# One hybrid decoder layer: the decay and rate low-rank products as 64-row pairs, begun later

## The chip, the cores and the metric

The kernel runs on one core of a Trainium2 chip, in one launch. The metric is the device time of that launch in microseconds (us), the median of several runs. Every engine of the core has its own queue of instructions: TensorE (PE, matrix products; PEld are its weight loads), VectorE (DVE), ScalarE (ACT), GpSimd (POOL) and SyncE (SP), which here mostly issues transfers (DMA). Engines wait for one another by semaphores, and each engine works its queue in order.

## The reference

One layer on 1024 tokens of 1024 channels, all in float32. Its first half mixes tokens in two branches that share one input projection:

```python
h = rms_norm(x, norm_mix_pre)
proj = h @ w_in            # r, k, v | decay down (64), rate down (64), gate down (128) | S5 input | two gates
p = token_shift(p, mu)     # p + (previous token - p) * mu
r, k, v, wd, ad, gd = split(p)
w = -softplus(-(w0 + tanh(wd) @ w2)) - 0.5
decay = exp(-exp(w))
a = sigmoid(a0 + ad @ a2)
g = sigmoid(gd) @ g2
```

`w2` and `a2` are 64 x 512, `g2` is 128 x 512: these are the three low-rank products. Decay, rate `a`, `k` and `v` drive a recurrence over tokens with a 64 x 64 state in each of 8 heads (RWKV-7); its output is normalised, gets a bonus term and is multiplied by `g`. The other branch is a diagonal complex state-space model (S5) with a gated output. Both branches are projected, merged with the two gates and projected once more; then follow a norm and the residual. The second half is a gated MLP with a causal convolution of width 3 and norms around it.

## The kernel before

The kernel holds activations with channels on the 128 partitions and tokens along the free dimension, in two halves of 512 tokens (`th` 0 and 1). A float32 product is made of three products in a reduced format: an operand is split into a high part (a cast on ScalarE) and a low part (a subtraction on VectorE), and high x high, high x low and low x high are summed in one PSUM bank (`mm3_steps`, L162). One such *step* has three products of 128 x 128 by 128 x 512. A projection tile (`inproj`, L943) is eight steps into one bank for each half of the tokens; `load_w` (L142) fetches its weights and splits them, into four buffers each for the high (`wh`) and the low part (`wl`).

Banks of the front half come from `gmp` (L95), four of them under the name `gm`. An evicted tile lies in one of four buffers `ev` (NEVA) until its store to device memory has landed.

The order of TensorE's instructions is that in which the program emits them; for the other engines and the transfers a scheduler orders instructions by priority and by when it expects them to be ready. `drive` (L185) emits that order: *lanes* (the S5 work first, the recurrence afterwards) run when a planned clock `now` has reached their due time, and in between `background` (L209) takes steps from a list of fill work. Each `yield` of a fill generator is the planned time that it adds to `now`: 0.68 for a step.

The first fill work is `mix_in` (L1122). It runs projection tile 12, which holds the decay and rate down-projections in its upper and lower 64 rows; `shifted_into` (L1080) applies the token shift, the tanh on the 64 decay rows, and splits the result into two `lx` buffers for each half. Then `rkv(0)` (L1113), three projection tiles of 16 steps each, is mixed with `lowrank` (L1095): after each third projection step one low-rank step. The decay weights are padded with 64 rows of zeros below and the rate weights with 64 rows of zeros above (L1962 to 1963), so each is a full 128-row product with the same `lx` operand: for each, four output tiles for two halves of the tokens, 16 steps in all. A decay tile is evicted by two ScalarE instructions (L1108, L1110), a rate tile by one (L1108), and stored to `TZ` or `TA`. The first low-rank step stands behind three projection steps. After it, tile 13 (the gate down-projection) and `rkv(1)`, mixed with the eight steps of the gate weights after each fourth projection step (`TG`). The rest of the fill work are `rkv(2)`, `rkv(3)`, sixteen gate tiles (`gate_tiles`, evicted at L1147), and later the merge of the branches and the output projection. The recurrence reads `TZ` and `TA` in `rwkv_front` (L641), and `TG` in `rwkv_out` (L900). Its products are 64-row ones, addressed by `HALF`, the upper and lower 64 partitions (L716, L850 and others). The output of its first 512 tokens goes through `YR` to the merge (L1196).

Of the kernel before, what the change touches and what calls it, by code (L numbers as in the profile page):

```python
# [12 lines left out]
AF = mybir.ActivationFunctionType  # L13
# [12 lines left out]
HALF = (slice(0, 64), slice(64, 128))  # L26
# [24 lines left out]
def _constants():  # L51
    c = np.zeros((128, NCST), np.float32)

    def put(name, a):
        o, n = CST[name]
        c[:, o:o + n] = a
    p = np.arange(128)
    put("ident", np.eye(128))
    s, t = (p % 64)[:, None], (p % 64)[None, :]
    put("gmask", np.where(p[None, :] < 64, s < t, s <= t))  # L60
    put("ones_bd", (p[:, None] // 64) == (p[None, :] // 64))
    put("nrow", np.broadcast_to(p[None, :], (128, 128)))
    put("smask", np.broadcast_to((np.arange(512) % 64 != 0)[None, :], (128, 512)))
    return c


class Kern:
# [1024 lines left out]
            self.split(*xs[-1], y)  # L1092
        return use

    def lowrank(self, xs, js):  # L1095

        nc = self.nc
        for j, hb, dst in js:
            w = self.load_w(self.a["w_lr"][j])
            for th in range(2):  # L1100
                for p in range(4):
                    ps = self.gmp()
                    yield from self.mm3_steps(ps, w, p, [xs[th][0]], [xs[th][1]])
                    t = self.ev()
                    if hb is None:
                        nc.scalar.copy(t, ps)
                    else:
                        nc.scalar.activation(t, ps, AF.Tanh, bias=self.hb[hb][:, p:p + 1], scale=0.5)  # L1108
                    if dst is self.TZ:
                        nc.scalar.activation(t, t, AF.Identity, bias=self.ones1, scale=1.0)  # L1110
                    nc.sync.dma_start(dst[p][:, th * 512:th * 512 + 512], t)

    def rkv(self, p):  # L1113

# [6 lines left out]

    def mix_in(self):  # L1122

        def mixed(a, b, n):

            for i, c in enumerate(a):
                yield c
                if i % n == n - 1:
                    c = next(b, None)
                    if c is not None:  # L1130
                        yield c
            yield from b
        self.load_u8(self.stored)
        xs = [[], []]
        yield from self.inproj((12, self.shifted_into(xs[0], 12)))
        yield from mixed(self.rkv(0), self.lowrank(xs[0], ((0, "w0", self.TZ), (1, "a0", self.TA))), 3)
        yield from self.inproj((13, self.shifted_into(xs[1], 13)))
        yield from mixed(self.rkv(1), self.lowrank(xs[1], ((2, None, self.TG),)), 4)
        self.mixed_in = True
        for p in (2, 3):  # L1140
            yield from self.rkv(p)
# [799 lines left out]
def _layout(i):  # L1941

    i = {k: np.asarray(v) for k, v in i.items()}
    f = {k: v[0] for k, v in i.items()}

    p = np.arange(512).reshape(4, 8, 16).transpose(0, 2, 1).reshape(-1)
    q = np.arange(f["w_in"].shape[1])
    q[14 * 128:18 * 128] = 14 * 128 + p
    f["w_in"] = f["w_in"][:, q]
    f["s5_w_glu"], f["s5_b_glu"] = f["s5_w_glu"][p][:, p], f["s5_b_glu"][p]  # L1950
    f["w_branch_s5"] = f["w_branch_s5"][p]

    def tiles(w):
        k, m = w.shape
        return np.ascontiguousarray(w.reshape(k // 128, 128, m // 128, 128).transpose(2, 1, 0, 3)).reshape(m // 128, 128, k)
    vec = {"g_mix_pre": f["norm_mix_pre"], "g_mix_post": f["norm_mix_post"], "g_ffn_pre": f["norm_ffn_pre"],
           "g_ffn_post": f["norm_ffn_post"], "b_gate": f["b_gate"], "mu": f["rwkv_shift_mu"], "w0": f["rwkv_w0"],
           "a0": f["rwkv_a0"], "k_k": f["rwkv_k_k"], "k_a": f["rwkv_k_a"], "r_k": f["rwkv_r_k"].reshape(-1),
           "lnx_w": f["rwkv_lnx_w"], "lnx_b": f["rwkv_lnx_b"], "b_glu": f["s5_b_glu"],
           "cw0": f["ffn_conv_w"][0], "cw1": f["ffn_conv_w"][1], "cw2": f["ffn_conv_w"][2], "cb": f["ffn_conv_b"]}  # L1960
    vec = np.concatenate([vec[n].reshape(-1, 128).T for n in VEC], axis=1)
    z = np.zeros((64, 512), np.float32)  # L1962
    lr = np.stack([np.concatenate([f["rwkv_w2"], z]), np.concatenate([z, f["rwkv_a2"]]), f["rwkv_g2"]])

    def dup(*xs):
        return np.stack([np.concatenate([x, x]) for x in xs])
    return {
        "x": np.ascontiguousarray(f["x"].T), "w_in": tiles(f["w_in"]), "vec": np.ascontiguousarray(vec),
        "cst": _constants(), "w_lr": lr, "w_glu": tiles(f["s5_w_glu"]),
        "w_br": np.stack([tiles(f["w_branch_rwkv"]), tiles(f["w_branch_s5"])]), "w_out": tiles(f["w_out"]),  # L1970
        "w_up": tiles(f["ffn_w_up"]), "w_down": np.ascontiguousarray(f["ffn_w_down"].reshape(FT, 128, D)),
        "s5_a": dup(f["s5_a_re"].T, f["s5_a_im"].T),
        "s5_ls": np.ascontiguousarray(np.broadcast_to(f["s5_log_step"][None], (128, 32))),
        "s5_b": dup(f["s5_b_re"].transpose(1, 0, 2), f["s5_b_im"].transpose(1, 0, 2)),
        "s5_c": dup(f["s5_c_re"].transpose(2, 0, 1), f["s5_c_im"].transpose(2, 0, 1)),
        "s5_d": np.ascontiguousarray(f["s5_d"].reshape(32, 16).T),
    }
# [19 lines left out]
```

## Time and profile before

| | |
|---|---|
| median of 3 runs | 1490.86 us (1490.47 to 1492.2) |
| span of the profiled execution, first to last instruction | 1491.1 us |
| TensorE busy | 1435.8 us (96%), 9284 products |
| VectorE busy | 1071.2 us (72%) |
| ScalarE busy | 729.8 us (49%) |
| mean granted clock of TensorE | 0.984 |
| transfers | 206.26 MB, mean 138 GB/s |

The profile gives the span of its one execution; beside it no separate time is recorded, and the runs lie within 1.1 us of it. In the profile's rows a group or instruction is named by engine, line of the program, operation and tiles (output <- inputs, with buffer numbers left out). "128*128 128x512" is a product of a 128 x 128 weight with 512 columns, "64*64" one in a quarter of the array. In a timeline a row has its start, its length (for several in a row, from the first start to the last end) and in brackets the idle time ahead of it and what ended it. Products overlap in the pipeline: the distance of two starts is what a product costs, and not its length. PEclk is the clock granted to TensorE, as a share of the full one.

### The profile page before, as it was taken

How to read it: one execution, taken by the hardware profiler on the slowest of the kernel's cores; microseconds unless marked ns; L12 is line 12 of the kernel's file. 1: busy time of each engine (PE TensorE's matmuls, PEld its weight loads, DVE VectorE, ACT ScalarE, POOL GpSimd, SP SyncE). 2: the span in 40 equal slices, each digit the busy share in tenths (PEclk: the TensorE clock that was granted, in tenths of full speed). 3: DMA queues.
4: the chain of work that ended last, by engine and by line, in shares of the span. 5: the costliest groups of instructions: out<-in, count | busy, mean ns of one | idle time of the engine just before them, and what ended most of it. 6: DMA issues, size and time to landing. Idle time of an engine off the chain costs nothing. (4 is left out here: it accounts for less than half of the span.)

```text
span 1491.1 us, 24155 instructions
## 1 busy us (share of the span) xinstructions
PE 1435.8 (96%) x9284; PEld 1176.3 (79%) x9284; DVE 1071.2 (72%) x1761; ACT 729.8 (49%) x1167; POOL 58.9 (4%) x116
## 2 busy tenths in 40 slices
PE   7999999999999989899999999999999999999996
PEld 5778888778878778677878877888888887888785
DVE  8977765665325859646597798777777777697677
ACT  7677653443324553633554455444444444443351
POOL 0000000010100110100000000000000000000001
PEclk9999999999999999899999999999999999999998
DMA  6453433633511575733374643222222227934723
GB/s 217 121 194 116 129 94 91 212 113 122 164 59 58 171 226 163 189 109 108 121 222 150 205 127 121 85 85 85 85 85 81 76 70 260 328 125 133 236 83 113
DMA packets 121284, 206.26 MB, mean 138 GB/s; under 512 B 29248, under 2 KB 35520, under 8 KB 121168
## 3 DMA queue, kind: packets, MB, share of 16 engines
q1 hardware_dynamic: 113296, 182.43, 39.2%
q0 software_dynamic: 6144, 19.99, 4.0%
q10 hardware_dynamic: 1728, 2.29, 0.4%
q8 instruction: 73, 1.20, 0.4%
q14 instruction: 43, 0.35, 0.1%
HBM read 150.14 MB, written 52.43 MB: 136 GB/s over the span
## 5 line engine op out<-in xcount | busy, mean ns | idle before, releaser
L172 PE MATMUL gm<-hh,wh 128*128 128x512 f32 x672 | 277.0, 412 | 10.5 <-DVE ev L1192 4.3
L173 PE MATMUL gm<-hl,wh 128*128 128x512 f32 x672 | 265.4, 395 | 0.0
L174 PE MATMUL gm<-hh,wl 128*128 128x512 f32 x672 | 265.2, 395 | 0.0
L156 ACT CAST wh<-wf 128x512 fp32r<-128x512 f32 x171 | 105.6, 619 | 168.3 <-PE gm L173 103.8
L157 DVE TENSOR_TENSOR wl<-wf,wh 128x512 fp32r<-128x512 f32 x171 | 116.9, 686 | 77.6 <-ACT wh L156 77.3
L172 PEld LDWEIGHTS gm<-hh,wh 128*128 128x128 f32 x672 | 127.6, 190 | 42.8 <-issue 5.9
L174 PEld LDWEIGHTS gm<-hh,wl 128*128 128x128 f32 x672 | 128.0, 190 | 28.1
L173 PEld LDWEIGHTS gm<-hl,wh 128*128 128x128 f32 x672 | 128.2, 191 | 24.7 <-issue 1.0
L1615 PE MATMUL d<-xl,wh 128*128 128x512 f32 x308 | 121.4, 394 | 3.5 <-DVE xl L227 3.5
L1614 PE MATMUL d<-xh,wh 128*128 128x512 f32 x308 | 121.4, 394 | 2.1 <-ACT xh L226 2.1
L1616 PE MATMUL d<-xh,wl 128*128 128x512 f32 x308 | 121.2, 393 | 0.0
L1440 PE MATMUL rp<-t,h 128*128 128x512 f32 x216 | 84.4, 391 | 1.6 <-ACT p L1454 1.6
L1442 PE MATMUL rp<-t,l 128*128 128x512 f32 x216 | 84.2, 390 | 0.5 <-DVE l L227 0.5
L1441 PE MATMUL rp<-t,h 128*128 128x512 f32 x216 | 84.1, 389 | 0.0
L1615 PEld LDWEIGHTS d<-xl,wh 128*128 128x128 f32 x308 | 58.6, 190 | 16.5 <-DVE xl L227 4.3
L1614 PEld LDWEIGHTS d<-xh,wh 128*128 128x128 f32 x308 | 58.5, 190 | 14.8 <-ACT xh L226 2.5
L1616 PEld LDWEIGHTS d<-xh,wl 128*128 128x128 f32 x308 | 58.6, 190 | 12.2
L226 ACT CAST h<-r 128x1024 fp32r<-128x1024 f32 x34 | 35.8, 1054 | 61.1 <-PE rp L1441 29.6
L227 DVE TENSOR_TENSOR l<-r,h 128x1024 fp32r<-128x1024 f32 x34 | 41.6, 1224 | 29.2 <-ACT h L226 27.7
L1461 DVE SCALAR_TENSOR_TENSOR y<-zv,vecs,y 128x1023 f32<-128x1023 f32 (+1 forms) x36 | 46.1, 1280 | 8.5 <-ACT y L1459 8.5
L1440 PEld LDWEIGHTS rp<-t,h 128*128 128x128 f32 x216 | 40.5, 188 | 11.2 <-ACT p L1454 2.5
L1454 ACT COPY p<-rp 128x512 f32<-128x512 f32 x54 | 31.0, 574 | 36.5 <-PE rp L1442 36.5
(459 smaller groups left out, 3199.4 us busy)
## 6 DMA issues: line engine op xcount, KB each, us to landing
r<-in_w_up_dram SPq DMA_DIRECT2D x36, 512.0 KB, 3.7
wf<-in_w_in_dram SPq DMA_DIRECT2D x62, 256.0 KB, 3.1
st<-in_w_down_dram SPq DMA_DIRECT2D x55, 256.0 KB, 4.1
st<-ACT SPq DMA_DIRECT2D x44, 256.0 KB, 4.5
wf<-in_w_up_dram SPq DMA_DIRECT2D x36, 256.0 KB, 2.9
ACT<-y POOLq DMA_DIRECT2D x18, 512.0 KB, 2.9
GT<-ev SPq DMA_DIRECT2D x32, 256.0 KB, 2.6
wf<-in_w_br_dram SPq DMA_DIRECT2D x32, 256.0 KB, 2.9
```

Of the source, the lines that this page charges most:

```text
L156: nc.scalar.copy(h[:, :n], f[:, :n])
L157: nc.vector.tensor_tensor(l[:, :n], f[:, :n], h[:, :n].bitcast(F32), ALU.subtract)
L172: mm(ps, a, xh[k], start=k == 0, stop=False)
L173: mm(ps, a, xl[k], start=False, stop=False)
L174: mm(ps, b, xh[k], start=False, stop=k == n - 1)
L1440: mm(ps, wh[:, c], xh, start=first and k == 0, stop=False, skip_group_check=True)
L1441: mm(ps, wh[:, c], xl, start=False, stop=False, skip_group_check=True)
L1442: mm(ps, wl[:, c], xh, start=False, stop=k == 3, skip_group_check=True)
L1461: V.scalar_tensor_tensor(y[:, lag:], z[:, 0:1024 - lag], self.vec(nme, i), y[:, lag:], ALU.mult, ALU.add)
L1614: mm(ps, wh[:, c], xh[:, x], start=start, stop=False, skip_group_check=True)
L1615: mm(ps, wh[:, c], xl[:, x], start=False, stop=False, skip_group_check=True)
L1616: mm(ps, wl[:, c], xh[:, x], start=False, stop=stop, skip_group_check=True)
```

## The change

The decay and rate weights stand in one 128 x 512 tile, decay in the upper 64 rows and rate in the lower ones, with no zeros. For each of the eight output tiles two banks are taken, and six products of 64 rows go out in turn to the upper and the lower half of the array: high x high for decay, high x high for rate, then the two other kinds. Both results are then evicted as before, by the function `lowrank_out`. A pair is planned at 0.9 us instead of two steps of 0.68. One weight tile less is loaded. In `mixed`, the low-rank generator is first taken at step 8 of the projections, where it loads its weights and gives no product; its products come after every third projection step from step 16 on, so the first one stands behind 19 projection steps (before: 3). The gate-rank products follow the same pattern (before: every fourth step from the start).

```diff
-    def lowrank(self, xs, js):
+    def lowrank_out(self, ps, hb, dst, p, th):
 
         nc = self.nc
...
+        t = self.ev()
+        if hb is None:
+            nc.scalar.copy(t, ps)
+        else:
+            nc.scalar.activation(t, ps, AF.Tanh, bias=self.hb[hb][:, p:p + 1], scale=0.5)
+        if dst is self.TZ:
+            nc.scalar.activation(t, t, AF.Identity, bias=self.ones1, scale=1.0)
+        nc.sync.dma_start(dst[p][:, th * 512:th * 512 + 512], t)
+
+    def lowrank_pair(self, xs):
+
+        mm = self.nc.tensor.matmul
+        (wh,), (wl,) = self.load_w(self.a["w_lr"][0])
+        yield 0
+        for th in range(2):
+            xh, xl = xs[th]
+            for p in range(4):
+                ps = self.gmp(), self.gmp()
+                o = slice(p * 128, p * 128 + 128)
+                for n, (a, b) in enumerate(((wh, xh), (wh, xl), (wl, xh))):
+                    for k, sl in enumerate(HALF):
+                        mm(ps[k], a[sl, o], b[sl], start=n == 0, stop=n == 2)
+                yield 0.9
+                self.lowrank_out(ps[0], "w0", self.TZ, p, th)
+                self.lowrank_out(ps[1], "a0", self.TA, p, th)
+
+    def lowrank(self, xs):
+
+        w = self.load_w(self.a["w_lr"][1])
+        yield 0
+        for th in range(2):
+            for p in range(4):
+                ps = self.gmp()
+                yield from self.mm3_steps(ps, w, p, [xs[th][0]], [xs[th][1]])
+                self.lowrank_out(ps, None, self.TG, p, th)
...
-        def mixed(a, b, n):
+        def mixed(a, b, lead, n):
 
             for i, c in enumerate(a):
                 yield c
-                if i % n == n - 1:
+                if i == lead // 2 or i >= lead and (i - lead) % n == n - 1:
...
-        yield from mixed(self.rkv(0), self.lowrank(xs[0], ((0, "w0", self.TZ), (1, "a0", self.TA))), 3)
+        yield from mixed(self.rkv(0), self.lowrank_pair(xs[0]), 16, 3)
...
-        yield from mixed(self.rkv(1), self.lowrank(xs[1], ((2, None, self.TG),)), 4)
+        yield from mixed(self.rkv(1), self.lowrank(xs[1]), 16, 3)
...
-    z = np.zeros((64, 512), np.float32)
-    lr = np.stack([np.concatenate([f["rwkv_w2"], z]), np.concatenate([z, f["rwkv_a2"]]), f["rwkv_g2"]])
+    lr = np.stack([np.concatenate([f["rwkv_w2"], f["rwkv_a2"]]), f["rwkv_g2"]])
```

More of the change, by code (lines that the diff above doesn't have):

```diff
@@ L1093, in shifted_into @@
         return use
-    def lowrank(self, xs, js):
+    def lowrank_out(self, ps, hb, dst, p, th):
         nc = self.nc
[L1098 to L1111, printed above, removed]
+        t = self.ev()
[29 more added lines that the diff above has]
+                self.lowrank_out(ps, None, self.TG, p, th)
     def rkv(self, p):
```

## Prediction

> **What bounds the kernel now.** I read the page first, then the busy time in stretches of 20 us, then the timeline of TensorE around the low-rank products. TensorE is the bound: it is busy in nearly every slice, also where the changed stage lies (slices 3 and 4 of 40, 37 us each).
>
> ```profile
> span 1491.1 us, 24155 instructions
> ...
> PE   7999999999999989899999999999999999999996
> ...
> PEclk9999999999999999899999999999999999999998
> ```
>
> Over the first 760 us it is busy for 727; the stretch from 60 to 80 us is one of the few with a hole.
>
> ```profile
> 60.00:80.00 20.00, 17.45 (x71) 13.33 (x70) 18.81 (x53) 15.77 (x22) 0.00 (x0) 0.97 0.77 211
> ...
> sum 760.00, PE 727.12 PEld 592.33 DVE 497.85 ACT 387.22 POOL 40.42; mean PE 19.13 PEld 15.59 DVE 13.10 ACT 10.19 POOL 1.06
> ```
>
> So time taken out of TensorE's own stream in the front half shifts everything behind it, as long as later work isn't waiting for something else. (The chain that ended last is followed back only through the last products of the kernel, and says nothing of this stage.) The timeline shows the hole:
>
> ```profile
> 74.20 0.39 PE L174 MATMUL gm<-hh,wl 128*128 128x512 f32 x1
> 76.50 0.51 PE L172 MATMUL gm<-lx,wh 128*128 128x512 f32 x1 [1.92 <-ACT lx L226]
> 77.52 0.50 PE L173 MATMUL gm<-lx,wh 128*128 128x512 f32 x1 [0.52 <-DVE lx L227]
> ...
> 78.80 0.63 PE L172 MATMUL gm<-hh,wh 128*128 128x512 f32 x1
> 79.22 0.63 PE L173 MATMUL gm<-hl,wh 128*128 128x512 f32 x1
> ...
> 82.20 0.40 PE L174 MATMUL gm<-lx,wl 128*128 128x512 f32 x1
> ...
> 87.24 0.39 PE L172 MATMUL gm<-lx,wh 128*128 128x512 f32 x1
> ...
> 89.96 0.39 PE L172 MATMUL gm<-lx,wh 128*128 128x512 f32 x1
> ```
>
> The rows that read `lx` are the low-rank products. From 87.24 to 89.96 lie 12 products of 512 columns: 2.72 us, so **0.227 us each and 0.68 us a step of three**. The first low-rank step stands after three projection steps of the next tile and waits for its split input. Then, from 78.80 on, products start 0.425 us apart; the granted clock says why:
>
> ```profile
> 74.60:76.50 1.90, 0.00 (x0) 0.00 (x1) 1.19 (x3) 1.85 (x4) 0.00 (x0) 1.00 0.63 254
> ...
> 78.80:82.20 3.40, 3.40 (x10) 2.63 (x8) 3.32 (x17) 0.90 (x2) 0.97 (x2) 0.50 0.42 166
> ```
>
> (columns: length, busy PE, PEld, DVE, ACT, POOL, clock, DMA share, GB/s). For 3.4 us after the wait the clock is 0.50.
>
> **The late start.** The product after 74.20 would have begun at 74.43. From there to 82.20 is 7.77 us for 14 products, which at 0.227 take 3.17: **4.6 us lost**, 3.0 to the waits and 1.6 to the clock. In the changed kernel the first low-rank product comes after 19 projection steps of the tile instead of 3, 10.9 us later, at about 72.2 + 12.9 = 85.1. Its inputs are ready by 79:
>
> ```profile
> 78.29 0.68 DVE L227 TENSOR_TENSOR lx<-ev,lx 128x512 fp32r<-128x512 f32 x1
> ```
>
> The projection steps that move ahead need their weights: those of the next tile were cast long before 72, as this row on ScalarE shows (two casts, the last two before 62).
>
> ```profile
> 59.83 1.14 ACT L156 CAST wh<-wf 128x512 fp32r<-128x512 f32 x2
> ```
>
> So I take the 4.6 us as gone. One low-rank weight load with its cast and its subtraction is gone too:
>
> ```profile
> L156 ACT CAST wh<-wf 128x512 fp32r<-128x512 f32 x171 | 105.6, 619 | 168.3 <-PE gm L173 103.8
> L157 DVE TENSOR_TENSOR wl<-wf,wh 128x512 fp32r<-128x512 f32 x171 | 116.9, 686 | 77.6 <-ACT wh L156 77.3
> ```
>
> That is 0.62 and 0.69 us on engines that were waiting for TensorE or for each other at such places, hidden by the products; uncovered it would be 1.3 us. I count nothing. The gate-rank steps (`TG`) move the same way, from every fourth step to every third behind a lead of 16; TensorE waits for `lx` nowhere but in the two rows above, and their eight stores, 5 us later in the SP queue, are read only at the output of the recurrence: nothing either way. The `TZ` and `TA` stores stay 16 and finish earlier.
>
> **The products.** Before: 16 steps of 0.68 = 10.9 us. After: 8 pairs of six 64-row products. Whether the two halves run at once, the trace shows only for narrower tiles:
>
> ```profile
> 397.17 0.27 PE L850 MATMUL cz<-V,gr 64*64 64x64 f32 x1
> 397.17 0.27 PE L851 MATMUL cz<-V,gr 64*64 64x64 f32 x1
> 397.18 0.27 PE L850 MATMUL cz<-V,gr 64*64 64x64 f32 x1
> 397.19 0.27 PE L851 MATMUL cz<-V,gr 64*64 64x64 f32 x1
> 397.27 0.22 PE L850 MATMUL cz<-V,gr 64*64 64x64 f32 x1
> ...
> 485.04 0.39 PE L174 MATMUL gm<-hh,wl 128*128 128x512 f32 x1
> 485.36 1.98 PE L716 MATMUL cz<-ar,bk 64*64 64x128 f32 x64
> 487.27 0.51 PE L172 MATMUL gm<-hh,wh 128*128 128x512 f32 x1
> 487.61 0.40 PE L173 MATMUL gm<-hl,wh 128*128 128x512 f32 x1
> ```
>
> Four products, one in each quarter of the array, start within 0.02 us, and in these lines of the code the upper and lower row halves do write the same columns, in two banks, as the new pair does. The 64 products of L716 have 128 columns each; by 0.227 us for 512 that is 0.057 us each, 3.63 us one after another, and the whole block takes 1.9. So the row halves do run at once, and the six products should take the time of three, 0.68 us. The same rows price the change between full and half rows: from 485.04 to 487.61 is 2.57 us, less two ordinary pitches 2.12, less the block at two at a time (1.81) leaves 0.3 us. A weight load of 128 columns instead of 64 is exposed with it, so I take 0.35 per pair, as eight separate blocks lie between projection steps. A pair is then 1.03 us, eight are 8.2, and the products **save 2.6 us**. Bounds: both halves at once and no price for changing, 8 x 0.68 = 5.4 us saved; one after another, 8 x (1.36 + 0.35) = 13.7 us, 2.8 lost. I stay near the first by the rows above.
>
> The Trainium skill (TensorE: Matmul & The Clock Gate, Measured speedup vs the span model) speaks for less: four row tiles of 512 columns gave 3.07 times, not four. At that share two halves give 1.54 times, an estimate of 0.88 us for the six products and 1.6 us less saved, 1486.8 in the end; L716 shows nothing of such a loss. The same page (HAM oscillation — how this bites in real kernels) lets the clock fall only after some 3.4 us of idle time; here waits of 1.92 and 0.52 us were followed by 0.50. If the rule held strictly, the 1.6 us of slow clock would have another cause and could stay, 1486.8 again; no run here shows another cause.
>
> **Evictions.** What was one eviction for each four steps is now two, issued together three steps later.
>
> ```profile
> L1072 ACT ACTIVATE ev<-gm,mu 128x512 f32<-128x512 f32 x9 | 6.2, 685 | 8.7 <-PE gm L174 4.3 <-issue 3.8 <-ACT t L569 0.5
> ...
> L1110 ACT ACTIVATE ev<-ev,ones 128x512 f32<-128x512 f32 x8 | 5.8, 724 | 0.2
> ...
> L1108 ACT ACTIVATE ev<-gm,hb_w 128x512 f32<-128x512 f32 x8 | 5.5, 682 | 1.2 <-PE gm L174 1.1
> ...
> L1108 ACT ACTIVATE ev<-gm,hb_a 128x512 f32<-128x512 f32 x8 | 5.3, 679 | 1.9 <-issue 1.9
> ```
>
> A pair costs ScalarE 0.68 + 0.72 + 0.68 = 2.08 us, in a period of three steps and a pair, 2.04 + 1.03 = 3.07. Over the eight pairs (24.6 us) ScalarE has 16.7 us of these, 3 x 0.69 for projection tiles and some 3 x 0.62 for weight casts: 20.6 of 24.6. It holds, with little to spare. A pair takes two of the four `gm` banks while a projection tile holds a third. The second bank of a pair comes free about 0.2 + 2.08 us after its last product, and the next pair wants it at 2.04; at the two pairs right behind a tile's end the old tile's bank isn't free either, and 0.69 us of its eviction may come between. That is 0 to 1.8 us; I take **0.5 us lost**, nearer the row of one eviction, where TensorE didn't wait at all. Behind it only the later projection steps would queue.
>
> **Sum up to the end of the front half:** -4.6 - 2.6 + 0.5 = -6.7 us.
>
> **Downstream.** The list of background steps is shorter by 16 x 0.68 - 8 x 0.9 = 3.7 planned us, so at each later fixed step of the recurrence about five more projection steps are already done. Where TensorE is full this changes nothing; but after the first half's output there is a place where it isn't:
>
> ```profile
> 525.76 0.60 PE L924 MATMUL rp<-csts,mt 128*128 128x128 f32 x4
> ...
> 543.95 0.50 PE L172 MATMUL gm<-hh,wh 128*128 128x512 f32 x1 [1.48 <-ACT ev L1147]
> ...
> 557.34 0.79 PE L172 MATMUL gm<-hh,wh 128*128 128x512 f32 x1 [2.70 <-ACT ev L1147]
> ```
>
> ```profile
> 533.30 0.62 ACT L226 CAST hh<-ld 128x512 fp32r<-128x512 f32 x1 [4.83 <-DMA ld<-YR]
> ...
> 539.26 1.33 ACT L226 CAST hh<-ld 128x512 fp32r<-128x512 f32 x2 [3.42 <-DMA ld<-YR]
> ...
> 543.25 0.64 ACT L1147 ACTIVATE ev<-gm,hb_b_gate 128x512 f32<-128x512 f32 x1
> ```
>
> ScalarE waits in order for the `YR` loads, which hang on the outputs of L924; the gate tile's eviction L1147 stands behind them, and TensorE waits for its bank. With 3.7 us of gate tiles already done, TensorE comes to that bank up to 3.7 us sooner against the same load. If the order on ScalarE stays, up to 3.7 us are given back; if the tile's eviction, ready sooner, goes ahead of the first wait of 4.83 us, nothing is, or the old 1.48 goes too. I take 1.0 lost (from -2 to 3.7). **Total -5.7 us**: 1491.1 - 5.7 = 1485.4 for the profiled execution, whose span is 0.2 above the median of the runs, so **1485.2** against 1490.86.
>
> **Rivals.** (1) *Given back at the output of the first half*: the full 3.7 us and one more stretch of half clock (1.6) instead of 1.0: -6.7 + 5.3, 1489.5. For it: the waits above; against it: the order on ScalarE is planned anew. (2) *The halves don't run at once*: the products lose 2.8 instead of saving 2.6, -4.6 + 2.8 + 0.5 + 1.0 = -0.3, 1490.6. Against it, the four starts within 0.02 us. (3) *Slower: the stores pace the pairs.* The four `ev` buffers are held until a store lands:
>
> ```profile
> DMA to landing us min/median/max: 2.0/3.5/5.9
> ```
>
> With landing time l a pair holds them for 2.08 + 2l, eight pairs and three projection tiles (twice 0.69 on two engines, + l each) for 21 + 19l, over four buffers 5.2 + 4.75l. At 3.5 that is 21.9 us, less than the 24.6 of the stretch. Above 4.1 every 0.1 costs 0.48 us, and the waits bring the half clock back (say twice, 3.2 us). With 7.2 won and 1.0 lost downstream the gain is used up at about 4.8, and the kernel is over 0.2% slower from 5.4 on; at the longest landing, 5.9, it is 33.2 - 24.6 + 3.2 + 1.0 = 12.8 lost against 7.2 won, 1496.5. Two stores every 3.07 us instead of one in 2.72 speak for it, a median of 3.5 against.
>
> **How the numbers follow.** Forecast (1482 to 1488) 0.58, and 0.05 for more than that (nearly free changing of modes, a lucky order downstream); rival 1 0.18; rival 2 0.07; rival 3 0.12. About 0.2%, 3 us, is what a measurement of this kernel can tell from no change. Faster is the forecast and the better tail, 0.63; within 0.2% rivals 1 and 2, 0.25; slower rival 3, 0.12. The range from 1480 to 1492.5 takes in the best products (-5.4) and rivals 1 and 2 and leaves out rival 3 and little else; the forecast's own is 1482 to 1488.
>
> **What would show it.** The low-rank pairs' rows should come in bunches with two starts together and the pair's six products within about 1.0 us; 1.7 or more is rival 2. No row on `lx` should wait for ScalarE near 75 us, and the clock from 74 to 85 should be 1.00; a wait there makes the 4.6 wrong. Waits of TensorE on `gm` for L1108 or L1110 with idle ScalarE before them are rival 3. The end of the first projection tiles should lie 6 to 7 us earlier; if it does and the kernel's end doesn't, look at the waits for L1147 between 520 and 560. A kernel within 3 us of before, or slower, makes the forecast wrong.

## The result, and the profile after

The changed kernel took 1501.83 us (median of 4 runs, 1497.72 to 1504.43) against 1491.13 of the kernel before: a ratio of **1.0071** (95% interval 1.0048 to 1.0094). It is slower by 10.7 us; 1485.2 was predicted, and 1501.83 lies above the range. The profiled execution took 1501.26 us, and its span is 1499.5 us.

The span is 8.4 us longer than the 1491.1 of before, with the same 9284 products. Where they are held up is seen in stretches of the timeline (columns: stretch, length, busy time of TensorE, its weight loads, VectorE, ScalarE and GpSimd, then TensorE's clock, DMA share, GB/s). Before:

```profile
72.00:85.00 13.00, 10.57 (x39) 7.95 (x38) 11.48 (x48) 7.15 (x11) 0.97 (x2) 0.87 0.59 176
85.00:110.00 25.00, 25.00 (x112) 20.71 (x111) 19.45 (x31) 20.71 (x34) 0.00 (x0) 1.00 0.59 197
...
540.00:590.00 50.00, 45.82 (x198) 37.11 (x198) 37.26 (x82) 29.25 (x53) 2.34 (x4) 0.93 0.61 177
...
740.00:790.00 50.00, 48.65 (x225) 40.29 (x224) 44.30 (x80) 24.75 (x43) 2.15 (x4) 1.00 0.68 211
```

The same stretches of the changed kernel:

```profile
72.00:85.00 13.00, 13.00 (x59) 10.77 (x59) 12.11 (x50) 6.57 (x12) 0.98 (x2) 1.00 0.59 183
85.00:110.00 25.00, 21.75 (x93) 14.35 (x92) 18.65 (x29) 19.15 (x30) 0.00 (x0) 0.93 0.53 181
...
540.00:590.00 50.00, 42.72 (x185) 34.65 (x184) 36.15 (x78) 28.44 (x52) 4.31 (x7) 0.93 0.60 179
...
740.00:790.00 50.00, 44.19 (x193) 36.31 (x194) 42.17 (x76) 23.68 (x42) 2.15 (x4) 0.97 0.59 189
```

The hole at the first low-rank step is closed (2.4 us more of busy time, and the full clock). Three others open: 3.3 us where the pairs now are, 3.1 us at the output of the first half of the tokens, 4.5 us at the merge. The list of TensorE's waits has a new or a grown row for each (columns: product and line, what it waited for, us in total, times, the longest):

```profile
PE gm L172 <- ACT ev L1168: 6.5, 2, 5.1
PE mm L172 <- ACT wh L156: 5.4, 1, 5.4
PE gm L1119 <- ACT ev L1102: 3.3, 3, 1.9
```

L1168 is the gate tile's eviction (L1147 before), L1119 a product of a pair, L1102 the eviction of a low-rank tile.

Three events divide the layer's first half: the first of the recurrence's 64-row products (L716), the last product of its output (L924), and the last store of the first half's normed result for the first 512 tokens (`H`), which is taken here as its end. The views of these lines give the first and the last start behind the durations. Before:

```profile
L716 PE MATMUL cz<-ar,bk x512: 268/269/321, 292.2 to 530.7; 64*64 64x128 f32 x171
...
L924 PE MATMUL rp<-csts,mt x32: 270/272/273, 511.4 to 721.6; 128*128 128x128 f32 x32
...
L1350 SPq DMA_DIRECT2D H<-tm x8: 319/323/327, 797.4 to 808.7; - x8
```

After:

```profile
L716 PE MATMUL cz<-ar,bk x512: 268/269/322, 297.1 to 533.8; 64*64 64x128 f32 x171
...
L924 PE MATMUL rp<-csts,mt x32: 270/272/418, 512.9 to 729.0; 128*128 128x128 f32 x32
...
L1371 SPq DMA_DIRECT2D H<-tm x8: 319/323/327, 805.1 to 816.4; - x8
```

The recurrence begins 4.9 us later, its last output comes 7.4 us later, and the first half ends 7.7 us later. So the time is lost in the first half of the layer; the remaining 0.7 us of the span lies behind it. No edit in this document touches that part, and in the profiled executions it takes from 677.0 to 683.1 us, so 0.7 us says nothing. In the experiments below these three events show where the time goes, and ratios over repeated runs on one chip give the verdicts.

### The profile page after: what moved, and what is told of

The parts are those of the page before. It is cut to its first block, busy times and chain, and to the rows that moved or that the text cites. A ratio compares the mean times of both kernels' runs of the same rounds, so it can differ in the third digit from the quotient of the medians.

```text
span 1499.5 us, 24143 instructions
## 1 busy us (share of the span) xinstructions
PE 1436.7 (96%) x9284; PEld 1173.2 (78%) x9284; DVE 1069.6 (71%) x1760; ACT 728.6 (49%) x1166; POOL 58.8 (4%) x116
## 5 line engine op out<-in xcount | busy, mean ns | idle before, releaser
L173 PEld LDWEIGHTS gm<-hl,wh 128*128 128x128 f32 x672 | 128.6, 191 | 24.6 <-issue 1.0
```

Source lines behind the costliest of these rows:

```text
L173: mm(ps, a, xl[k], start=False, stop=False)
```

## The front half: what the rows show

A pair in the changed kernel (timeline of TensorE and of its weight loads):

```profile
85.87 0.39 PE L174 MATMUL gm<-hh,wl 128*128 128x512 f32 x1
...
86.19 0.50 PE L1119 MATMUL gm<-lx,wh 64*128 64x512 f32 x2
...
86.52 0.40 PE L1119 MATMUL gm<-lx,wh 64*128 64x512 f32 x2
86.76 0.40 PE L1119 MATMUL gm<-lx,wl 64*128 64x512 f32 x2
87.08 0.50 PE L172 MATMUL gm<-hh,wh 128*128 128x512 f32 x1
87.42 0.40 PE L173 MATMUL gm<-hl,wh 128*128 128x512 f32 x1
```

Two products start together, three times; the halves run at once. From 85.87 to 87.42 is 1.55 us; without two ordinary pitches (0.453) the pair costs **1.10 us**, eight 8.8. In the middle the couples are 0.24 us apart (86.52 to 86.76), nearly the 0.227 of one full product. At the change into half rows and at the change back a start comes some 0.1 us late, twice each time.

From the third pair on, TensorE waits for banks (timeline of TensorE and ScalarE):

```profile
91.17 0.31 ACT L517 ACTIVATE sml<-sml 64x128 f32<-64x128 f32 x1 [2.10 <-DVE sml L513]
...
93.78 0.69 ACT L1102 ACTIVATE ev<-gm,hb_w 128x512 f32<-128x512 f32 x1 [1.17 <-DMA RKV<-ev]
94.78 0.69 ACT L1102 ACTIVATE ev<-gm,hb_a 128x512 f32<-128x512 f32 x1 [0.31 <-DMA TA<-ev]
...
94.52 0.50 PE L1119 MATMUL gm<-lx,wh 64*128 64x512 f32 x1 [1.95 <-ACT ev L1102]
95.52 0.73 PE L1119 MATMUL gm<-lx,wh 64*128 64x512 f32 x3 [0.50 <-ACT ev L1102]
```

The second pair was finished at about 90.3, and its evictions began at 93.78. ScalarE first stood 2.10 us before L517, an instruction of the state-space tables that waits for VectorE, then evicted a projection tile, then waited 1.17 us for a store to free an `ev` buffer. Behind the wait the clock is halved:

```profile
96.58:99.30 2.72, 2.72 (x7) 2.15 (x7) 2.69 (x5) 2.28 (x3) 0.00 (x0) 0.50 0.85 312
```

How much of the front half's gain is left is seen on VectorE, from the token shift of tile 12 to that of tile 13, with the three mixed tiles between. Before, and then after:

```profile
72.10 0.74 DVE L1073 SCALAR_TENSOR_TENSOR ev<-gm,vecs,ev 128x511 f32<-128x511 f32 x1
...
130.54 0.74 DVE L1073 SCALAR_TENSOR_TENSOR ev<-gm,vecs,ev 128x511 f32<-128x511 f32 x1
```

```profile
72.91 0.75 DVE L1073 SCALAR_TENSOR_TENSOR ev<-gm,vecs,ev 128x511 f32<-128x511 f32 x1
...
130.09 0.75 DVE L1073 SCALAR_TENSOR_TENSOR ev<-gm,vecs,ev 128x511 f32<-128x511 f32 x1
```

That is 58.44 us and 57.18: 1.3 us gained, where 6.7 had been predicted. It explains a smaller gain and no loss; the loss comes later.

## The experiments

All of these kernels compute the whole layer. The kernel before took 1487.2 to 1487.3 us (medians of 22 to 35 runs) on the chips of the experiments; every ratio is to the kernel before on the same chip. First the measured events of all profiled executions in one place, in us (the last column is the distance of the second and the third event). Each row is one execution, and executions of one kernel differ: that of `plan_kept` was the fastest of its ten runs (1487.81 us), that of `pairs_spread` the slowest (1501.46). In the other kernels a run's time is 1.8 us above its span; by that the profiled execution of the kernel before took some 1493 us (an estimate), 5 to 6 above its medians here. So a single distance of a few us is weak evidence; the ratios and what holds over groups of rows are better.

```
kernel                    recurrence   last     last store   output
                          begins       output   of the half  to store
before                    292.2        721.6    808.7        87.1
after                     297.1        729.0    816.4        87.4
lead_only                 291.0        717.6    804.7        87.1
pairs_spread              293.5        728.9    817.1        88.2
plan_kept                 292.4        715.1    808.6        93.5
plan_only                 299.3        732.1    813.8        81.7
slot_only                 293.6        717.2    810.8        93.6
slot_undone               296.0        732.3    814.0        81.7
plan_and_slot             293.4        717.5    804.6        87.1
plan_slot_period4         287.9        714.3    801.4        87.1
shift_late                298.1        730.0    815.8        85.8
plan_slot_ev5             289.8        716.5    803.6        87.1
plan_slot_lead6_period5   291.3        718.3    805.5        87.2
```

### One part alone: the late start, and the pairs

`lead_only` is the kernel before with its 16 full-row low-rank steps, begun late:

```diff
-                if i % n == n - 1:
+                if i >= lead and (i - lead) % n == n - 1:
...
-        yield from mixed(self.rkv(0), self.lowrank(xs[0], ((0, "w0", self.TZ), (1, "a0", self.TA))), 3)
+        yield from mixed(self.rkv(0), self.lowrank(xs[0], ((0, "w0", self.TZ), (1, "a0", self.TA))), 16, 2)
```

> The products as in the kernel before (16 full-row steps, planned 0.68 each), only begun behind 17 projection steps instead of 3 and then after every second one; the gate-rank steps are untouched. Theory P (the planned time of the background work is what cost the 10 us: it is unchanged here): the wait for lx and the half clock behind it are gone, 3 to 4.6 us, 1486.5 to 1488. Rival S (beginning the low-rank work later is itself harmful, since its stores and evictions then fall together): slower than before, 1493 or more.

Measured: 1484.56 us, ratio 0.9975 (0.9957 to 0.9993); the first half ends 4.0 us sooner. From the token shift of tile 12 to that of tile 13 it takes 55.29 us in place of 58.44, 3.1 gained; two waits of 0.23 and 0.90 us for its own low-rank weights, which this kernel fetches only when their first step is due, cost it 1.1. The late start is worth not far below what was predicted for it, and is not what harms.

`pairs_spread` is the changed kernel with its pairs spread from the start, one after every sixth projection step:

```diff
-        yield from mixed(self.rkv(0), self.lowrank_pair(xs[0]), 16, 3)
+        yield from mixed(self.rkv(0), self.lowrank_pair(xs[0]), 0, 6)
```

> Pairs as in the changed kernel, planned 0.9 us each, but without a lead, one after every sixth projection step, so the evictions have twice the time. Theory P (planned time): the planned time is as short as in the changed kernel, so the loss downstream stays, 1496 to 1502, although no wait for ev should show among the pairs. Rival E (the buffers ev in the stretch of pairs are the cause): the loss goes, 1486 to 1490.

Measured: 1494.12 us, ratio 1.005 (1.0027 to 1.0074). The waits of the pairs for L1102 shrink to one of 0.29 us (two of 0.48 and 0.43 us are for VectorE), and the recurrence begins only 1.3 us later than before; still its last output comes 7.3 us later, and the waits for L1168 (6.6 us) and of `mm` for `wh` (5.2 us) stay. The time lies between the two expectations; what paces the pairs isn't the main loss.

### The planned time

`drive` lets a lane take a step only when its credit isn't negative, and credit grows by the planned time of fill steps:

```python
if self.fill and self.credit < 0:
    continue
...
self.credit = min(self.credit + c, CREDIT)
```

A pair planned at 0.9 earns 0.46 less than the two steps that it replaces, eight pairs 3.7 less. `plan_kept` gives it back, with all else as changed:

```diff
-                yield 0.9
+                yield 1.36
```

> The changed kernel with each pair planned at 1.36 us, the planned time of the two steps that it replaces; what the engines compute is unchanged. Theory P: the order of the later stages is again that of before, and what is left is the front half's own sum, 4.6 of waits and clock and 2.2 of products saved against 3.3 of eviction waits and 1.6 of clock lost: about 1489, 1487 to 1491. Rival E (eviction waits) or S (late start): as the changed kernel, 1498 to 1503.

Measured: 1492.16 us, ratio 1.0033 (1.0013 to 1.0053), half of the loss. The recurrence begins at 292.4, as before, and its last output comes at 715.1, 13.9 us sooner than in the changed kernel and 6.5 sooner than before. But between that and the store the kernel takes 93.5 us in place of 87.1. A wait of the list fills that:

```profile
PE mm L172 <- ACT wh L156: 5.3, 1, 5.3
...
PE gm L172 <- ACT ev L1168: 2.3, 2, 1.2
```

The wait for L1168 is back to less than before (4.2); the one of `mm` isn't. Two causes, then, and the plan is one.

`plan_only` is the kernel before, with the planned time of its 16 steps lowered by the same 3.7 and nothing else:

```diff
-                    yield from self.mm3_steps(ps, w, p, [xs[th][0]], [xs[th][1]])
+                    for _ in self.mm3_steps(ps, w, p, [xs[th][0]], [xs[th][1]]):
+                        yield 0.68 if j == 2 else 0.45
```

> The kernel before with its 16 decay and rate steps planned at 0.45 us instead of 0.68, 3.7 us less in all; products, evictions and their places among the projection steps are unchanged. Theory P: the background work runs ahead of the recurrence as in the changed kernel and the loss at the output of the first half and at the change of pools comes back, 1496 to 1502. Rivals E and S: as before, 1490 to 1492.

Measured: 1498.13 us, ratio 1.006 (1.0032 to 1.0087). With no product changed, a shorter planned time alone makes the kernel 0.6% slower. The recurrence begins 7.1 us later and its last output comes 10.5 us later; of that 5.4 us is recovered before the store (81.7 instead of 87.1). There is no wait of `mm` for `wh` in its list.

### The staging buffer

The wait of `mm` in the changed kernel (timeline of TensorE, SyncE, VectorE and ScalarE):

```profile
744.92 0.80 PE L172 MATMUL mm<-e,wh 128*128 128x512 f32 x1 [5.43 <-ACT wh L156]
...
723.66 2.91 SPq L155 DMA_DIRECT2D wf<-in_w_br_dram  x2
...
741.52 6.23 SPq L155 DMA_DIRECT2D wf<-in_w_br_dram  x6
...
740.81 0.69 DVE L1344 TENSOR_TENSOR et<-ev,ev 128x512 f32<-128x512 f32 x1 [4.74 <-ACT ev L1342]
...
744.25 2.18 ACT L156 CAST wh<-wf 128x512 fp32r<-128x512 f32 x4 [3.48 <-DMA wf<-in_w_br_dram]
```

and the same place before:

```profile
738.20 0.50 PE L172 MATMUL mm<-e,wh 128*128 128x512 f32 x1 [0.68 <-ACT mx L1316]
...
718.84 3.72 SPq L155 DMA_DIRECT2D wf<-in_w_br_dram  x2
```

Both kernels load two merge weights early. In the changed one the weight that the first product needs isn't among them: it is loaded with the six from 741.52 on. `load_w` says why that can be:

```python
self.wfs = (self.wfs + 1) % (2 if self.wfp is None else 4)
f = (self.wp, self.wfp)[self.wfs // 2].tile([128, 512], F32, tag="wf", ...)
```

A counter deals the raw weights in turn to the buffers of two pools. At the merge the second pool (`wfx`) opens in memory that the work before it uses until its last sum of squares (L1344, to 741.50); the six loads are issued 0.02 us later, and the view of the DMA queue's own waits names what they waited for (in the kernel before it is L1323, 5.9 us):

```profile
SPq L155 <- DVE et L1344: 5.1, 1, 5.1
```

The packed tile needs one load fewer; the counter is one step behind for all loads that follow, and the first merge weight falls on a buffer of the late pool.

`slot_only` is the kernel before, with the counter moved by one at the decay weights:

```diff
+            if j == 0:
+                self.wfs = (self.wfs + 1) % 2
```

> The kernel before with nothing changed but the counter that hands out the staging buffers of weights: it is moved on by one, once, ahead of the low-rank loads, as the missing load of the changed kernel moves it. Theory W (with one load fewer the first merge weight after the first half falls on a staging buffer of a pool that opens only when the front half is over): a wait of about 5.3 us for that weight at the first product of the last merge, with half clock behind it 1.6 us, so 5 to 7 us slower than before, ratio 1.0035 to 1.0045. Rival (the load count is indifferent; the wait in the changed kernel came from the planned time or the late start): as before, ratio 0.999 to 1.001.

Measured: 1493.23 us, ratio 1.0043 (1.0026 to 1.006). The wait is there, at the same size:

```profile
PE mm L172 <- ACT wh L156: 5.4, 1, 5.4
```

`slot_undone` is the changed kernel with the counter moved back at the packed weights:

```diff
         mm = self.nc.tensor.matmul
+        self.wfs = (self.wfs + 1) % 2
         (wh,), (wl,) = self.load_w(self.a["w_lr"][0])
```

> The changed kernel with that counter moved on by one, so that the buffers fall as in the kernel before. Theory W: the wait of 5.4 us and its half clock go, 5 to 7 us less than the changed kernel, ratio to before 1.002 to 1.004, the rest being the planned time. Rival (load count indifferent): as the changed kernel, 1.006 to 1.008.

Measured: 1492.13 us, ratio 1.003 (1.0016 to 1.0044). The wait is gone, and output to store is 81.7 us instead of 87.4. The other wait stays, for L1169 (L1168, one line further on): 6.3 us in two, the longer one 4.8. Adding or taking away one step of the counter makes and unmakes the wait. By the last column of the table it costs 5.7 to 6.5 us, and that column is steady: 87.1 or 87.2 in all six kernels with plan and counter as before, 93.5 and 93.6 in the two with the plan as before and the counter out of step.

`plan_and_slot` has both repairs, the counter's line and `yield 1.36`:

> The changed kernel with both: pairs planned at 1.36 us and the counter moved on by one. Theory P and W together: what is left is the front half's own sum, and the last norm of the mixing half is written 5 to 8 us earlier than before; ratio 0.995 to 0.9975, near the run with the late start alone. Rival (the pairs cost something else that isn't found): at or above before, 0.999 or more.

Measured: 1485.59 us, ratio 0.9983 (0.9969 to 0.9998); the first half ends 4.1 us sooner than before. Faster than before, though by less than expected. From the changed kernel's 1.0071 (measured on another chip) the counter alone takes 0.0041, the plan alone 0.0038, both together 0.0088: the two account for the sign. What is left between this and the forecast (0.9962 as a ratio) is in size the wait of the pairs, 3.2 us here, with slow clock behind it:

```profile
93.03 0.50 PE L1120 MATMUL gm<-lx,wh 64*128 64x512 f32 x1 [1.45 <-ACT ev L1102]
94.09 0.73 PE L1120 MATMUL gm<-lx,wh 64*128 64x512 f32 x3 [0.56 <-ACT ev L1102]
...
94.60:97.50 2.90, 2.90 (x9) 2.05 (x8) 2.90 (x4) 1.54 (x3) 0.00 (x0) 0.58 0.57 208
```

### The pairs' own wait

`plan_slot_period4` has both repairs and a pair after every fourth projection step:

```diff
-        yield from mixed(self.rkv(0), self.lowrank_pair(xs[0]), 16, 3)
+        yield from mixed(self.rkv(0), self.lowrank_pair(xs[0]), 16, 4)
```

> As the run with planned time and counter both restored, with the pairs after every fourth projection step instead of every third. Theory E (the evictions of a pair hold the four ev buffers too long, 3.3 us of waits and 1.6 of half clock): these go, another 3 to 5 us, ratio 0.992 to 0.995. Rival (those waits are hidden later anyway): as the run before it, 0.995 to 0.9975.

Measured: 1482.1 us, ratio **0.9966** (0.9952 to 0.9979), the lowest of all; the expected gain was larger. The waits for L1102 fall to two of 0.49 us (with one of 0.36 for VectorE's eviction), the clock from 80 to 100 us is 1.00, and the first half ends 7.3 us sooner than before.

`plan_slot_lead6_period5` begins earlier and spreads more (`16, 3` becomes `6, 5`):

> As the run with planned time and counter both restored, but the lead is 6 steps and a pair stands after every fifth projection step (the first behind 11 steps, when the split input is just ready by the trace of before). Theory: the evictions have 4.5 us for each pair and neither the wait for lx nor that for ev shows, so it is at or below the run with period 4: 0.994 to 0.9965. Rival (the input isn't ready, or evictions fall together with the tables of the other branch): above it, 0.997 or more.

Measured: 1483.35 us, ratio 0.9979 (0.9967 to 0.9991): the waits for L1102 come to 1.9 us (1.2 of the pairs, 0.7 of projection steps), and those for L1169 to 4.7. Spreading further brought nothing more.

`plan_slot_ev5` asks whether the four `ev` buffers set the pace; both repairs, and

```diff
-NEVA = 4
+NEVA = 5
```

> As the run with planned time and counter both restored, pairs after every third step, but with five ev buffers instead of four in the front half. Theory E (the waits of a pair's bank for ScalarE come from ScalarE waiting for a store to free an ev buffer): the 3.2 us of waits go and the half clock between 80 and 100 us with them, 3 to 5 us before the run with four, ratio 0.994 to 0.997. Rival (the bound is ScalarE's own time or the banks): waits of 2 us or more stay, ratio 0.997 to 1.0.

Measured: 1486.3 us, ratio 0.9986 (0.9971 to 1.0), as without the fifth buffer; the waits for L1102 come to 4.1 us, not less. Its timeline (ScalarE, TensorE):

```profile
89.27 0.31 ACT L517 ACTIVATE sml<-sml 64x128 f32<-64x128 f32 x1 [2.52 <-DVE sml L513]
...
91.23 1.31 PE L1120 MATMUL gm<-lx,wh 64*128 64x512 f32 x4 [1.54 <-ACT ev L1102]
...
104.35 0.95 PE L1120 MATMUL gm<-lx,wh 64*128 64x512 f32 x4 [1.92 <-ACT ev L1102]
```

None of these evictions waits for a store any more. At the first wait they stand in ScalarE's queue behind L517, which waits 2.52 us for VectorE. At the second ScalarE is simply busy: from 100.37 to 103.6 it has two copies of the state-space tables (L538 and L539, 1.05 and 1.06 us), a weight cast and the eviction of a projection tile. With one reason of the late eviction removed, others take its place.

### Giving the planned time back later

If the loss of the plan were only TensorE's arrival at one gate bank (L1168), the missing 3.7 could be given back just ahead of it. `shift_late` is `slot_undone` with that:

```diff
     def merge_loads(self):
         self.merge_load()
-        yield 0
+        yield 3.68
```

> The changed kernel with the staging counter put right and the pairs still planned at 0.9 us, but with 3.68 us of planned time added once, much later: in the empty step between gate tile 13 and the last two gate tiles, just ahead of the output of the recurrence's first half. Nothing else is changed. Theory P1 (the planned time matters because the last two gate tiles and the merge run ahead of that output): the alignment is restored there, the 6 us of waits for the evictions of gate tiles shrink to about 3 and the ratio is that of the run with both restored, 0.997 to 0.9995. Rival P2 (the order of everything between the low-rank steps and that point matters too): most of the loss stays, 1.001 to 1.004.

Measured: 1495.3 us, ratio 1.0053 (1.0037 to 1.0069), no better than `slot_undone` and above both expectations. The waits for L1169 are gone from the list, and another stands in their place: L822, a product of the recurrence, waits 5.0 us for ScalarE (L231). The recurrence begins at 298.1 here too. So the gate bank is where the lateness showed in the changed kernel, and not its only price. The trial is not an exact return of the 3.7, though: credit is capped at 2.0 (`CREDIT`, in the line `min(self.credit + c, CREDIT)` above), so one step of 3.68 can lift it to 2.0 at most.

## Why the prediction was wrong, point by point

**The late start (-4.6).** Right in its mechanism. No product waits for `lx`, the clock from 72 to 85 us is 1.00, and the stretch holds 20 more products than before, 4.5 us at 0.227. Alone (`lead_only`) it gained 3.1 us by VectorE's rows and moved the end of the first half by 4.0 us.

**The products (-2.6).** The mechanism is right, the size a little off: 1.10 us a pair, not 1.03, so 2.1 us saved. The rate at which halves run beside each other was right (0.24 against 0.227); the price of changing is 0.42 us a pair, not 0.35. The estimate that the prediction drew from the Trainium skill (TensorE: Matmul & The Clock Gate, Measured speedup vs the span model), 0.88 us for six products, is met as a number: 86.19 to 87.08 is 0.89. The rows show it as late starts at the changes, and the couple in the middle ran at the full rate.

**Evictions (0.5 lost, at most 1.8).** Mis-sized: 3.3 us of waits and 1.6 of half clock, 4.9. The count of ScalarE's work (20.6 us of 24.6) was the wrong question: it had 23.6 us of work in the 31.4 us from the first pair to the last, and left out the other branch's tables. ScalarE works in order; a pair's evictions stand behind an instruction that waits 2.10 us for VectorE, and then behind a store. With it the three terms of the front half come to -4.6 - 2.1 + 4.9 = -1.8, against the 1.3 us gained by VectorE's rows.

**"I count nothing" for the removed load.** This step failed. The prediction asked what the cast and the subtraction cost, and whether they were hidden. It didn't ask who else uses what the load advances: a counter shared by all later loads. One load fewer at 70 us made a wait of 5.43 us at 745 us, with half clock behind it: 5.7 to 6.5 us.

**Downstream (1.0 lost, -2 to 3.7).** The step that failed with it. The prediction saw that the fill list is 3.7 planned us shorter, and took it that this "changes nothing" where TensorE is full. But planned time is what the recurrence is released by. It was released 4.9 us later in the changed kernel and 7.1 in `plan_only`; and it also took longer. From its first 64-row product to its last output, the five kernels with the shorter plan take 431.9 to 436.3 us, the kernel before and the seven others 422.7 to 429.4. The whole price was 5.1 us at the end of the first half in `plan_only`, and 7.8 and 9.4 in the two pairs that differ by the plan (changed kernel and `plan_kept`, `slot_undone` and `plan_and_slot`), one execution each; by the ratios it is 0.6%, 0.38% and 0.47%, or 8.9, 5.7 and 7.0 us. The place the prediction named is one where it shows:

```profile
554.36 0.68 ACT L1168 ACTIVATE ev<-gm,hb_b_gate 128x512 f32<-128x512 f32 x1
...
555.08 0.79 PE L172 MATMUL gm<-hh,wh 128*128 128x512 f32 x1 [5.13 <-ACT ev L1168]
...
557.81 1.91 PE L747 MATMUL cz<-csts,bk 128*128 128x128 f32 x8
...
562.29 0.18 DVE L784 COPY mt<-mt 128x31 f32<-128x31 f32 x1 [4.82 <-ACT mt L783]
```

Here the eviction of the gate tile stands in ScalarE's queue behind work on loaded tiles, as the prediction said; the two waits are 6.5 us instead of 4.2. The rows also show part of why the recurrence itself takes longer. Its transposes (L747) come behind the wait in TensorE's order, and so does the product (L762) whose result ScalarE copies out at L783. On that hangs a chain of small VectorE operations: L784, then the inversion for the second 512 tokens, L789. In the kernel before L747 stands ahead of the longer wait:

```profile
548.17 1.03 PE L747 MATMUL cz<-csts,bk 128*128 128x128 f32 x8
```

From the last product of L716 to that chain's first L789 it takes 27.8 to 28.8 us in the changed kernel, `pairs_spread`, `plan_only` and `slot_undone`, and 22.2 to 24.8 in the nine others. `shift_late` is one of these nine (22.2): there this place is relieved, and the time is lost later, at L822 among others. What would keep the waits away stays open.

**The rivals.** Rival 1, the gain given back at the output of the first half, had the place and not the size: it stopped at 1489.5, having counted the 3.7 us once and no later start of the recurrence. Rival 2 falls with the starts in couples. Rival 3, the only slower one, isn't what happened. It decided from a landing time of 4.8 us on; the stores of the low-rank tiles landed within 2.0 to 4.2 us, with a median of 2.3. `pairs_spread`, with nearly no such wait, is slower all the same, and a fifth buffer changed nothing. The result is on the side of rival 3 by mechanisms that no rival had. With the two unforeseen ones undone and the pairs given a step more (`plan_slot_period4`) the change is worth 5.2 us (1487.28 to 1482.1), near the forecast's 5.7. How much of that the pairs bring beside the late start, the ratios don't tell: 0.9966 and 0.9975 (`lead_only`) have overlapping intervals. By VectorE's two token shifts it is 0.8 us (54.47 against 55.29), one execution each. That the gate-rank steps (`TG`) moved too was never tried alone; all kernels with pairs have it.

## What to carry to other kernels

In a kernel whose order comes from planned times and shared counters, a part that is removed or made shorter can move more than its own time: look up who counts with it. A planned time is an instruction to the scheduler as well as an estimate; when a step gets faster, change its time in one edit and its plan in another, and measure both. For an eviction, ask what stands ahead of it in its engine's queue before asking how busy the engine is.

## What was not expected of the hardware

**The clock after short waits.** TensorE's clock fell to half for about 3 us after waits of 1.95 and 0.50 us with half a microsecond of products between them (changed kernel), of 1.45 and 0.56 (`plan_and_slot`, 0.58 above), and of 1.92 and 0.52 (before). After one wait of 1.92 us alone it didn't (`plan_slot_ev5`, the stretch behind 104.35):

```profile
104.35:109.00 4.65, 4.65 (x27) 3.60 (x28) 0.29 (x2) 3.21 (x6) 0.00 (x0) 1.00 0.85 316
```

Behind a single wait of 2.70 us (before, 557.30 to 561.00) it was 0.50. So the longest wait alone doesn't decide it: 1.45 with 0.56 lowered the clock, and 1.92 didn't. The Trainium skill (TensorE: Matmul & The Clock Gate, HAM oscillation — how this bites in real kernels) lets the clock fall after some 3.4 us without work; in these rows less was enough. What the limit is, these runs don't show.

**Weight loads at a change of shape.** The weight loads of a pair start with its first product and not ahead of it, and the next full-row load waits likewise (view of the weight loads, changed kernel):

```profile
86.19 0.30 PEld L1119 LDWEIGHTS gm<-lx,wh 64*128 64x128 f32 x4 [0.35 <-issue]
...
87.08 0.19 PEld L172 LDWEIGHTS gm<-hh,wh 128*128 128x128 f32 x1 [0.37 <-issue]
```

At both changes no load runs ahead for some 0.35 us; that goes with the 0.42 us that a pair costs above its 0.68. The Trainium skill (TensorEngine Tiling (Array Packing), Key Properties) says that changing the tiling mode drains TensorE; the rows agree with it, and give the price here: 0.42 us for a change and the change back. That the late weight loads are its cause is a reading of these rows and wasn't tried.
